# A hybrid attention and SSD kernel: the SSD chunks are turned over, and TensorE's order in the scan is fixed

## The chip, the cores and the metric

The kernel runs on one core of one Trainium2 chip. The metric is the device time of one execution in microseconds. A core has TensorE (PE in the profile, with its weight loads as PEld), VectorE (DVE), ScalarE (ACT), GpSimd (POOL) and SyncE (SP), which issues most of the DMAs. Each engine works through its own queue in order; semaphores make one engine wait for another. TensorE reads its two operands, the stationary and the moving one, from SBUF and writes to PSUM.

## The reference, cut to what matters

Two layers act on 1024 latent tokens and 256 context tokens of width 1024. Layer 0 is windowed attention and is not touched. Layer 1 is a bidirectional Mamba-2 SSD mixer with 8 groups of 4 heads; a head has 64 channels, a state 128 rows. The latent tokens are cut into 8 chunks of 128. In the reference's names, for one direction:

```python
a_cs = jnp.cumsum(da, axis=2)
states = jnp.einsum('bcsgn,bcsgr,bcsgrp->bcgrpn', bm, decay_to_end, xdt)
h = jnp.exp(al)[..., None, None] * h + st                 # scan over the chunks
lmat = jnp.exp(jnp.where(lower, diff, -jnp.inf))
cb = jnp.einsum('bcqgn,bcsgn->bcqsg', cm, bm)
y_diag = jnp.einsum('bcqsg,bcqsgr,bcsgrp->bcqgrp', cb, lmat, xdt)
y_off = jnp.einsum('bcqgn,bcgrpn,bcqgr->bcqgrp', cm, h_prev, jnp.exp(a_cs))
```

and after both directions:

```python
y = y_f + y_b + d_skip * xs
u = rms_normalize((y * silu(z)).reshape(bsz, n, SSD_GROUPS, SSD_WIDTH // SSD_GROUPS))
out = (u.reshape(bsz, n, SSD_WIDTH) * norm_w) @ w_out
```

The gate z, the inputs xs, bm and cm come from one projection of the layer's input; xs, bm and cm go through a convolution over 5 tokens and a SiLU first. The RMS norm of u runs over the 256 channels of a group, token by token.

## The kernel before

All projections are done in split precision: an operand is cut into a high and a low part in fp32r, and three products are summed. The products of the scan are plain fp32; the profile shows each as two passes (two records).

**The stages.** After layer 0 the method `ssd` first runs the front of group 0, then a loop over the groups `g`, in it a loop over the chunks `c`. In the loop over the chunks, `slot` computes chunk `n = 8g + c` of group `g`, and between its parts a call `fill(x)` lets the generator `front(g + 1, ...)` issue projections of the next group. In the last group the generator is `ssd_out`, the output projection. So TensorE always has two kinds of work: the scan of this group, and *fillers* that belong to the next stage. Each filler yields its cost in microseconds (`N512` and `N256`), and `fill` stops at a share of the whole (`FRONT`) given by `SEGS`.

**The front of a group** projects four tiles of 128 channels over all tokens, in the order B, two halves of x, C (L1152 for the latent tokens, L1143 for the context, except C). The result lies in PSUM (`pj2`, two buffers, or `psD`, one buffer) and is convolved by ScalarE (L1034, the middle tap) and VectorE (L1038, the other four), then passed through tanh (L1045) and a product (L1046). B and x are also wanted with the tokens on partitions; for this TensorE transposes the tile into the PSUM space that it came from (L1085), and ScalarE copies it out (L1088). Last comes the gate z (L1177) with the tokens on the output partitions: the stationary operand is the input, the moving one the weight, 256 columns at a time. L1185 and L1188 make the SiLU.

These steps off TensorE are not issued at once. They are put in a `Queue`, `post`, which issues them while fillers run; an entry with a time (`LATE`) is issued that many microseconds of filler later.

**The states.** `states` is a generator for the backward chain: products of B and weighted x (`xw` from GpSimd, L1213) at L1236, a decay of the last state on GpSimd (L1218) and VectorE's sum (L1248), first for the context chunks in both directions, then for the latent chunks from the last to the second. `tick` takes one step of it. The forward state is carried inside `slot` (L1291, L1292).

**A chunk in `slot`** has the queries q on the output partitions. The scores (L1282) are multiplied into the decay matrix M (`fd`, L1286; M comes from `decays`: rows of the cumulated decay loaded from DRAM, one predicated copy L1270 and four exponentials L1272). The two inter-chunk products take C as the stationary operand and the states, 256 columns, as the moving one (L1284, L1285); VectorE scales the result by `eacs`, a factor per token and head (L1295). The diagonal takes M of a head as the stationary operand and 64 channels of x as the moving one (L1311). The skip term, a factor per token and head (`sk`), is multiplied into x on GpSimd (L1306) and added (L1307, L1308). VectorE adds the diagonal (L1320) and multiplies by the gate (L1321); ScalarE sums the squares (L1323), GpSimd takes the power -1/2 (L1324), ScalarE scales (L1329). In the next slot, `tail` transposes the chunk into channel-major form (L1341), ScalarE evicts it with the norm's weight (L1342), and a DMA writes it to `uN_d`.

**What sets the order.** The program is scheduled ahead of time: a timeline model orders the instructions of each engine, so an engine's queue may differ from the program's order. Nothing holds TensorE to the program's order.

**Output projection.** `ssd_out` loads the features from `uN_d` (`oraw`), splits them into high and low (L1529 and the subtraction after it), and multiplies by the weights (L1571). After the scan the rest of it and the final norm run.

## Time and profile before

| | |
|---|---|
| median of 3 runs | 1818.71 us (1813.79 to 1822.03) |
| the profiled execution, its time | 1818.37 us |
| its span, first to last instruction | 1816.6 us |
| mean granted TensorE clock | 0.99 |
| busy share: PE, PEld, DVE, ACT, POOL | 96%, 83%, 64%, 48%, 45% |
| DMA | 227.9 MB, 125 GB/s over the span |
| layer 0 and the joining stage | 0 to about 797 us of the span |
| scan with fronts, groups 0 to 6 | about 857 to 1595 us, 105.5 us per group |
| last group with the output projection | about 1595 to 1700 us |
| rest of the output projection, final norm | about 1700 to 1816 us |

A line of the profile's groups reads: source line, engine, operation, tile written and tiles read, shapes, count, then busy time in us and mean ns of one, then the idle time of the engine before them and what ended it. A matmul's record covers its way through the array, so records overlap; how fast TensorE goes is read from the distance of starts. In the chain of waits a piece has its start, its length and what it was. A line of the busy time by stretches has the stretch, its length, the busy time of PE, PEld, DVE, ACT and POOL with the number of instructions, the granted clock, the DMA engines' share and GB/s.

### The profile page before, as it was taken

To read this page: it belongs to the slowest core of one execution; us is meant where nothing else is said; L and a number is where in the kernel's file an instruction comes from. 1 tells how busy PE (TensorE), PEld (TensorE's weight loads), DVE (VectorE), ACT (ScalarE), POOL (GpSimd) and SP (SyncE) were. 2 spreads that over 40 slices of the span, in tenths; PEclk is the share of its full clock that TensorE was granted. 3 is DMA by queue.
4 is the path that set the end of the run, shared out by engine and by line. 5 is a ranking of instruction groups with operands and counts; after the bars stand their busy time and mean duration, and the time that the engine had idled before them with its cause. 6 is when DMAs were issued, how large, how long until landed. Compare 5 with 4: busy or idle time off the path is not lost.

```text
span 1816.6 us, 29129 instructions
## 1 busy us (share of the span) xinstructions
PE 1749.0 (96%) x10379; PEld 1500.2 (83%) x10379; DVE 1166.0 (64%) x2125; ACT 869.9 (48%) x1895; POOL 811.1 (45%) x1074
## 2 busy tenths in 40 slices
PE   6999998999999899999999999999999999999997
PEld 3797767788889687778898898989889898988886
DVE  3563536786787766675766748567675857766643
ACT  3521235677788766352444434344353434544522
POOL 2441127554456465303454544646454454644311
PEclk9999999999999999999999999999999999999998
DMA  8768865543345445311322323323332322655542
GB/s 296 285 156 255 261 192 138 119 116 99 99 117 132 118 133 195 112 42 52 86 68 79 93 69 88 82 71 79 78 93 78 82 79 74 188 163 179 163 137 70
DMA packets 209393, 227.89 MB, mean 125 GB/s; under 512 B 16096, under 2 KB 149088, under 8 KB 208224
## 3 DMA queue, kind: packets, MB, share of 16 engines
q1 hardware_dynamic: 175184, 207.38, 38.1%
q0 software_dynamic: 34064, 18.65, 5.6%
q8 instruction: 82, 1.34, 0.3%
q14 instruction: 63, 0.52, 0.1%
HBM read 191.14 MB, written 35.13 MB: 125 GB/s over the span
## 4 chain that ended last, share of the span: by engine, by line
PE 83%; DVE 5%; ACT 4%; DMA 4%; issue 3%; POOL 0%; SPq 0%; DVEq 0%; ACTq 0%; POOLq 0%
PE pj L1152 17%; PE pj L1177 10%; PE pj L1571 7%; PE pj L223 6%; PE pj L225 6%; PE pj L224 6%; PE psD L1143 3%; PE pt L694 3%; PE psX L1311 2%; PE pv L701 2%; PE psD L1236 2%; PE pv L700 2%; PE S L669 2%; PE psX L1285 1%; PE S L670 1%
## 5 line engine op out<-in xcount | busy, mean ns | idle before, releaser
L223 PE MATMUL pj<-uH,wh 128*128 128x256 f32 (+1 forms) x652 | 233.5, 358 | 8.1 <-DVE rope_b L532 2.3
L224 PE MATMUL pj<-uL,wh 128*128 128x256 f32 (+1 forms) x652 | 220.1, 338 | 0.0
L225 PE MATMUL pj<-uH,wl 128*128 128x256 f32 (+1 forms) x652 | 220.1, 338 | 0.0
L211 POOL TENSOR_TENSOR wl<-wr,wh 128x512 fp32r<-128x512 f32 x92 | 121.7, 1326 | 97.4 <-ACT wh L209 96.9
L1152 PE MATMUL pj<-uH,wh 128*128 128x512 f32 x480 | 161.4, 410 | 2.0 <-ACT xn L1088 1.2
L1152 PE MATMUL pj<-uH,wl 128*128 128x512 f32 x480 | 158.5, 403 | 0.0
L1152 PE MATMUL pj<-uL,wh 128*128 128x512 f32 x480 | 157.3, 402 | 0.0
L699 DVE TENSOR_TENSOR pl<-pt,ph 128x512 fp32r<-128x512 f32 x168 | 114.2, 687 | 61.3 <-ACT ph L698 60.4
L223 PEld LDWEIGHTS pj<-uH,wh 128*128 128x128 f32 x652 | 124.7, 191 | 34.9 <-issue 8.6
L1177 PE MATMUL pj<-wh,uH 128*128 128x256 f32 x512 | 148.0, 289 | 3.1 <-ACT xn L1088 3.0
L1177 PE MATMUL pj<-wl,uH 128*128 128x256 f32 x512 | 150.7, 294 | 0.0
L1213 POOL TENSOR_TENSOR xw<-xn,dtdec 128x256 f32<-128x256 f32 x144 | 92.9, 649 | 127.1 <-PE psD L1236 108.5
L1177 PE MATMUL pj<-wh,uL 128*128 128x256 f32 x512 | 149.5, 292 | 0.0
L1342 ACT ACTIVATE uT<-psX,nw 128x128 f32<-128x128 f32 x128 | 46.7, 365 | 193.2 <-PE psX L1341 193.1
L225 PEld LDWEIGHTS pj<-uH,wl 128*128 128x128 f32 x652 | 124.4, 191 | 14.8 <-issue 1.7
L673 DVE CUSTOM_DVE_ANT_0 sm<-S,mask,nsink 128x640 f32<-128x640 f32 (+2 forms) x160 | 118.7, 772 | 26.5 <-PE S L670 14.5
L224 PEld LDWEIGHTS pj<-uL,wh 128*128 128x128 f32 x652 | 124.9, 192 | 11.5 <-issue 2.8
L209 ACT CAST wh<-wr 128x512 fp32r<-128x512 f32 (+1 forms) x132 | 84.8, 645 | 102.5 <-PE pj L224 78.7
L698 ACT CAST ph<-pt 128x512 fp32r<-128x512 f32 x168 | 97.5, 585 | 64.5 <-PE pt L694 58.9
L675 ACT ACTIVATE sm<-sm,nm 128x640 f32<-128x640 f32 (+2 forms) x160 | 118.5, 742 | 12.6 <-DVE nm L673 12.3
L1152 PEld LDWEIGHTS pj<-uL,wh 128*128 128x128 f32 x480 | 90.1, 188 | 19.0
L1152 PEld LDWEIGHTS pj<-uH,wh 128*128 128x128 f32 x480 | 89.1, 188 | 19.6 <-ACT bn L1088 2.0
(383 smaller groups left out, 4999.8 us busy)
## 6 DMA issues: line engine op xcount, KB each, us to landing
fd<-acs SPq DMA_DIRECT2D x64, 256.0 KB, 5.0
bd<-acs SPq DMA_DIRECT2D x64, 256.0 KB, 5.2
wr<-w_x SPq DMA_DIRECT2D x31, 512.0 KB, 3.8
wr<-w_sk SPq DMA_DIRECT2D x24, 512.0 KB, 4.0
wr<-wg SPq DMA_DIRECT2D x44, 256.0 KB, 4.6
qs<-q POOLq DMA_DIRECT2D x40, 256.0 KB, 3.9
wr<-wo SPq DMA_DIRECT2D x40, 256.0 KB, 2.7
wada<-w_ad SPq DMA_DIRECT2D x8, 1024.0 KB, 6.4
```

The source lines that it names most:

```text
L211: (eng or nc.vector).tensor_tensor(l, raw, h, op=ALU.subtract)
L223: self.nc.tensor.matmul(ps, lh, rh, start=first and i == 0, stop=False)
L224: self.nc.tensor.matmul(ps, lh, rl, start=False, stop=False)
L225: self.nc.tensor.matmul(ps, ll, rh, start=False, stop=last and i == n - 1)
L673: nc.vector.tensor_tensor_reduce(out=sm[:, :W], in0=Sv, in1=self.mask[:, m0 : m0 + W], scale=-SCALE, scalar=self.nsink[:, 4 * j + r : 4 * ...
L675: nc.scalar.activation(sm[:, :W], sm[:, :W], AF.Exp, bias=nm[:, r : r + 1], scale=-1.0, accum_out=sums[:, r : r + 1])
L698: nc.scalar.copy(ph, ptf)
L699: nc.vector.tensor_sub(pl, ptf, ph)
L1152: nc.tensor.matmul(raw[:, 512 * i : 512 * i + 512], l[:, k, :], r[i][:, k, :], start=k + y == 0, stop=k == KT - 1 and y == 2)
L1177: nc.tensor.matmul(pj[:, c], l, r[:, k, :], start=c % 2 + q + k + y == 0, stop=c % 2 == 1 and q == 1 and k == 3 and y == 2)
L1213: nc.gpsimd.tensor_tensor(xw, X(st, c).rearrange("p (r h) -> p r h", r=R), self.dtdec[:, c, hd(d, g)].unsqueeze(2).broadcast_to([P, R, HP] ...
L1571: nc.tensor.matmul(banks[x], l[:, z, sl], r, start=k == 2 * qs[0] and y == 0, stop=k == 2 * qs[-1] + 1 and y == 2)
```

## The change

- *z turned over* (`front`): the weight tile is stationary, the input moves, 512 columns at a time, so z has channels on partitions. The layout of `w_z` follows. In each tile the latent tokens now come before the context.
- *Chunks turned over* (`scores`, `inter`, `state`, `diagonal` instead of `slot`): y has channels on partitions and queries along the free axis. The inter-chunk products take the states as stationary and C as moving operand, four of 128 columns. The diagonal takes 64 channels of x as the stationary and M as the moving operand; the four heads write to the lower and the upper 64 partitions by turns. The factor per token is no longer per partition, so `exp` of the cumulated decay goes to DRAM (`eacs_d`) and is loaded per chunk, broadcast over 64 partitions (`load_scale`, tile `eb`, two DMAs).
- *Diagonal on VectorE:* the skip term is added into M: four times the identity times `sk`, plus M.
- *Gate on GpSimd:* y times z moves from VectorE to GpSimd. Squares stay on ScalarE; GpSimd adds the two halves and a product with a column of ones gives the sum over channels. The power -1/2 is taken for four chunks at once and written to DRAM (`rn_d`). The chunk is stored before the norm; no transpose is left in the tail.
- *Norm in the output projection:* each feature tile is multiplied on GpSimd by the broadcast row of `rn_d`; the norm's weight is applied in the two splitting steps.
- *TensorE in program order:* `pin` links every TensorE instruction of groups 0 to 6 to the one before it in the program, beginning after the first chunk's scores, state and inter-chunk products.
- *Even fillers, states one by one:* four `fill` calls per chunk with new `SEGS`; the chain of states takes a step whenever `PACE_S` of filler has passed, inside `run`; its rest comes at the end of the last chunk. Transposes of the convolved tiles come `LATE` = 12 (context: `CLATE` = 9.2) us of filler after their tile, and the queue's timed entries are kept sorted.

```diff
-FRONT = 4 * 48 * N512 + 3 * 24 * N256 + 8 * 24 * N256
+FRONT = 4 * 48 * N512 + 3 * 24 * N256 + 4 * 24 * N512
 OUT = 4 * 30 * 3 * N512
 POST = 0.5
 DTLATE = 40.0
-LATE = 3.0
-SEGS = (1.5, 2.0, 2.0, 2.2, 2.2)
+LATE = 12.0
+CLATE = 9.2
+PACE_S = 1.85
+SEGS = (2.6, 2.4, 2.2, 2.25)
...
-            self.late.extend((self.now + f[0], x) for x in f[1])
+            self.late = deque(sorted([*self.late, *((self.now + f[0], x) for x in f[1])], key=lambda v: v[0]))
...
+        for d in range(2):
+            for f in range(2):
+                for r in range(R):
+                    row = 64 * d + 32 * f + r
+                    nc.sync.dma_start(self.eacs_d[r % 2, :, d, r // 2, 512 * f : 512 * f + 512], acs[row : row + 29 : 4, :512])
...
+    def pin(self, first):
+
+        traced = self.nc.cur_bb.bb.instructions
+        start = next(k for k in reversed(range(len(traced))) if traced[k] is first) + 1
+        last = None
+        for i in traced[start:]:
+            if i.engine == mybir.EngineType.PE:
+                if last is not None:
+                    self.tc.add_manual_dep(i, last.name, mybir.DependencyInfo(mybir.DependencyClass.NoSync, mybir.DependencyReason.DATA), reason="pin")
+                last = i
...
-            return [(LATE, steps)]
+            return [(late, steps[::2] + steps[1::2])]
...
+                acc2 = t(pf, [P, CTX], F32, "cctx")
+                post.extend(self.taps(x, raw2, acc2, 0, CTX, CTX) + self.silu(raw2, acc2) + natural(raw2, acc2, [(st[nat[0]][2], 0, 2)], nat[1], 2, CLATE))
+                if kind == 1:
+                    post.append((CLATE, [lambda: st.setdefault("ctx", True)]))
...
-            pj = t(ps, [P, 4, 256], F32, "pj2")
+            pj = t(ps, [P, 2, 512], F32, "pj2")
             for q in range(2):
                 ww = (w0, w)[q]
                 need(ww)
-                for c in range(4):
-                    for k in range(4):
-                        u, v = uH[i][:, 4 * q + k, c * P : (c + 1) * P], uL[i][:, 4 * q + k, c * P : (c + 1) * P]
-                        for y, (l, r) in enumerate(((u, ww["h"]), (u, ww["l"]), (v, ww["h"]))):
-
-                            nc.tensor.matmul(pj[:, c], l, r[:, k, :], start=c % 2 + q + k + y == 0, stop=c % 2 == 1 and q == 1 and k == 3 and y == 2)
-                            yield N256
+                for k in range(KT):
+                    for y, (l, u) in enumerate(((ww["h"], uH), (ww["h"], uL), (ww["l"], uH))):
+                        nc.tensor.matmul(pj[:, q], l[:, k, :], u[i][:, k, :], start=k + y == 0, stop=k == KT - 1 and y == 2)
+                        yield N512
...
+        def load_scale(n):
+            if n < G * NCH:
+                g, c = divmod(n, NCH)
+                x = eb[n] = t(ps2, [P, 2, 2, P], F32, "eb")
+                for f in range(2):
+                    src = self.eacs_d[f : f + 1, g, :, :, c * P : (c + 1) * P].rearrange("o d e q -> o (d e) q")
+                    nc.sync.dma_start(x[64 * f : 64 * f + 64].rearrange("p d e q -> p (d e) q"), src.broadcast_to([64, R, P]))
...
+        def scores(n, st, cur):
             g, c = divmod(n, NCH)
             cs = slice(c * P, (c + 1) * P)
             pcb = t(ps, [P, 512], F32, "psX")[:, :P]
             nc.tensor.matmul(pcb, st["bT"][:, cs], st["cT"][:, cs], start=True, stop=True)
+            M = cur["M"]
+            y2 = cur["y2"] = t(ps2, [P, 2, 2, P], F32, "y2")
+            sk = t(ps2, [P, R + 1], F32, "sk")
+            dg, sk = sk[:, R:], sk[:, :R]
+            nc.vector.tensor_tensor_reduce(out=y2[:, 0, 0], in0=pcb, in1=self.ident, scale=1.0, scalar=0.0, op0=ALU.mult, op1=ALU.add, accum_out=dg)
+            nc.vector.scalar_tensor_tensor(sk, in0=self.dtb[:, c, 4 * g : 4 * g + 4], scalar=dg, in1=self.dsk[:, 4 * g : 4 * g + 4], op0=ALU.mult, op1=ALU.add)
             nc.vector.tensor_tensor(M, M, pcb.unsqueeze(1).broadcast_to([P, R, P]), op=ALU.mult)
+            for r in range(R):
+                nc.vector.scalar_tensor_tensor(M[:, r], in0=self.ident, scalar=sk[:, r : r + 1], in1=M[:, r], op0=ALU.mult, op1=ALU.add)
+
+        def inter(n, st, cur):
+            g, c = divmod(n, NCH)
+            cs = slice(c * P, (c + 1) * P)
+            po = t(ps, [P, 2, 2, P], F32, "psX")
+            for d, h in enumerate((cur["hf"], st["hb"][c])):
+                for e in range(2):
+                    nc.tensor.matmul(po[:, d, e], flat(h)[:, e * P : (e + 1) * P], st["cT"][:, cs], start=True, stop=True)
+            y2 = cur["y2"]
+            nc.vector.tensor_tensor(y2, po, eb.pop(n), op=ALU.mult)
+            y = cur["y"] = t(ps2, [P, 2, P], F32, "yt")
+            cur["yadd"] = nc.gpsimd.tensor_tensor(y, y2[:, 0], y2[:, 1], op=ALU.add).ins
+
+        def state(n, st, cur):
+            g, c = divmod(n, NCH)
+            cur["hf"] = st["hf"]
             if c < NCH - 1:
+                xw = xweight(st, g, c, 0)
                 S = t(ps, [P, 512], F32, "psX")
                 hn = t(ps2, [P, R, HP], F32, "hf")
                 decay(hn, st["hf"], g, c, 0)
+                yield
+                nc.tensor.matmul(S[:, :256], B(st, c), flat(xw), start=True, stop=True)
                 nc.vector.tensor_add(hn, hn, S[:, :256].rearrange("p (r h) -> p r h", r=R))
                 st["hf"] = hn
+            yield
+
+        def diagonal(n, st, cur):
+            g, c = divmod(n, NCH)
+            cs = slice(c * P, (c + 1) * P)
+            M, y, y2 = cur["M"], cur["y"], cur["y2"]
             yd = t(ps, [P, 512], F32, "psX")
             for r in range(R):
+                e, f = divmod(r, 2)
+                nc.tensor.matmul(yd[64 * f : 64 * f + 64, e * P : (e + 1) * P], X(st, c)[:, r * HP : (r + 1) * HP], M[:, r], start=True, stop=True)
+            yadd = nc.vector.tensor_add(y, y, yd[:, :256].rearrange("p (e q) -> p e q", e=2))
+            nc.gpsimd.tensor_tensor(y, y, st["sz"][c], op=ALU.mult)
+            nc.sync.dma_start(self.uN_d[g][:, :, cs].rearrange("e p n -> p e n"), y)
+            nc.scalar.activation(y2[:, 0], y, AF.Square, scale=1.0 / 16.0)
+            sq = t(ps2, [P, P], F32, "sq")
+            nc.gpsimd.tensor_tensor(sq, y2[:, 0, 0], y2[:, 0, 1], op=ALU.add)
+
+            def tail():
+                pt = t(ps, [P, 512], F32, "psX")
+                nc.tensor.matmul(pt[:, :1], sq, self.ones[:, :1], start=True, stop=True)
+                if c % 4 == 0:
+                    self.ss = t(ps2, [P, 4], F32, "ss", 2)
+                ss = self.ss
+                nc.scalar.activation(ss[:, c % 4 : c % 4 + 1], pt[:, :1], AF.Identity, bias=self.eps4)
+                if c % 4 == 3:
+                    nc.gpsimd.tensor_tensor(ss, ss, self.mhalf, op=ALU.pow)
+                    nc.sync.dma_start(self.rn_d[g][c // 4].rearrange("o (c p) -> p (o c)", c=4), ss)
+
+            return tail, yadd.ins
 
...
-        st["xw"] = xweight(st, 0, 0, 0)
-        self.tail = None
+        cur = {"M": decays(0)}
+        scores(0, st, cur)
+        for _ in state(0, st, cur):
+            pass
+        inter(0, st, cur)
+        tail = None
+        traced = nc.cur_bb.bb.instructions
+        first = traced[-1]
...
+                    self.pin(first)
...
+                        if g < G - 1 and "ctx" in nst:
+                            chain = chain or states(g + 1, nst)
+                            if spent - mark > PACE_S and (steps < 4 or 1 in nst):
+                                next(chain, None)
+                                steps += 1
+                                mark = spent
...
+                    if n + 1 < G * NCH:
+                        load_scale(n + 2)
+                    if n + 1 < G * NCH:
+                        with self.tc.issue_after(cur["yadd"]):
+                            offset(n + 1)
+                    ntail, ydone = diagonal(n, st, cur)
+                    if tail:
+                        tail()
+                    tail = ntail
+                    load_rows(n + 2, 0)
+                    if n + 1 < G * NCH:
+                        with self.tc.issue_after(ydone):
+                            cur = {"M": decays(n + 1)}
+                    fill(0)
+                    if n + 1 == G * NCH:
+                        run(total * (c + 1) / NCH)
+                        break
+                    if c == NCH - 1:
+                        while not all(x in nst for x in ("bT", "cT", 1)) or not nst["sz"]:
+                            post.pop()
+                        st = nst
+                    scores(n + 1, st, cur)
+                    fill(1)
+                    fs = state(n + 1, st, cur)
+                    next(fs)
+                    if c < NCH - 1:
+                        inter(n + 1, st, cur)
+                        fill(2)
+                        for _ in fs:
+                            pass
+                    else:
+                        fill(2)
+                        for _ in chain:
+                            pass
+                        next(fs)
+                        inter(n + 1, st, cur)
+                    fill(3)
...
+                if k % 2 == 0:
+                    nc.sync.dma_start(scales[k // 2 % 2][:, k // 4 % 2 * 512 :][:, :512], self.rn_d[k // 2][i].broadcast_to([P, 512]))
...
+                def scale():
+                    nc.gpsimd.tensor_tensor(feats[n], feats[n], scales[k // 2 % 2][:, k // 4 % 2 * 512 :][:, :512], op=ALU.mult)
+
+                def high():
+                    nc.scalar.activation(hi, feats[n], AF.Copy, scale=self.nw[:, k : k + 1])
 
                 def low():
-                    nc.vector.tensor_sub(lo, feats[n], hi)
+                    nc.vector.scalar_tensor_tensor(lo, in0=feats[n], scalar=self.nw[:, k : k + 1], in1=hi, op0=ALU.mult, op1=ALU.subtract)
                     ready.add(order[n])
 
-                post.extend([lambda: nc.scalar.copy(hi, feats[n]), low])
+                post.extend([scale, high, low])
```

130 lines of the change are left out of this document (30 added, 100 removed).

## The prediction

> **What bounds the kernel now.** I read the page's head first, then busy time by stretches of one group of the scan stage, then the chain of waits.
>
> ```profile
> span 1816.6 us, 29129 instructions
> PE 1749.0 (96%) x10379; PEld 1500.2 (83%) x10379; DVE 1166.0 (64%) x2125; ACT 869.9 (48%) x1895; POOL 811.1 (45%) x1074
> ```
>
> ```profile
> 1067.07:1172.61 105.54, 104.80 (x652) 93.79 (x651) 71.96 (x123) 45.34 (x106) 53.67 (x75) 1.00 0.29 78
> ```
>
> The columns after the length are PE, PEld, DVE, ACT and POOL busy, then clock and DMA. TensorE is busy 104.8 of 105.5 us at full clock, so a group idles only 0.74 us. A busy PE may still be a slow one, so I look at the cadence.
>
> ```profile
> 1156.49 2.63 PE pj L1177 x22
> 1159.12 0.22 PE psX L1282 x2
> 1159.34 0.43 PE psD L1236 x2
> 1159.77 0.43 PE psX L1284 x2
> ```
>
> ```profile
> 1126.93 0.40 PE L1152 MATMUL pj<-uL,wh 128*128 128x512 f32 x1
> 1127.16 1.00 PE L1311 MATMUL psX<-xn,fd 128*128 128x64 f32 x8
> 1127.97 0.48 PE L1152 MATMUL pj<-uL,wh 128*128 128x512 f32 x1
> 1128.29 0.39 PE L1152 MATMUL pj<-uH,wl 128*128 128x512 f32 x1
> 1128.52 0.27 PE L1341 MATMUL psX<-ident,y 128*128 128x128 f32 x1
> 1128.55 0.47 PE L1152 MATMUL pj<-uH,wl 128*128 128x512 f32 x1
> 1128.86 0.63 PE L1152 MATMUL pj<-uH,wh 128*128 128x512 f32 x2
> ```
>
> The first fence is the chain of waits (start, length, what). It is nothing but TensorE, one piece starting where the last ended: 22 products of 256 columns take 2.63 us, 0.1195 each. The second is TensorE's timeline, with starts in the first column. A 512-column product takes 0.23 (1128.29 to 1128.52). From 1126.93 to 1128.29 there are two such products and the eight passes of the diagonal, so these cost 1.36 - 0.46 = 0.90 us. A transpose costs 1128.86 - 1128.29 - 0.46 = 0.11. Work put between the projections costs its own passes and no more, so in this stage a pass saved is time saved, and a wait of TensorE is time lost. There are almost no waits to remove.
>
> **The change part by part: TensorE's work.** The gate z is turned over: per group 192 products of 256 columns become 96 of 512.
>
> ```profile
> 1717.40 11.04 PE pj L1571 x48
> ```
>
> This piece of the chain (output projection, a new stationary tile each time) gives 0.230 per 512 columns. So 192 x 0.1195 = 22.9 becomes 96 x 0.230 = 22.1 us: 0.8 to 0.9 less per group, and over eight groups -7.0 us. It can hardly be worth less than 4.
>
> The diagonal: four products of 64 columns, bound by loading M, become four of 128 columns with X stationary, 64 columns wide, two on the lower and two on the upper half of the output partitions. A fp32 pass over 128 columns is 0.11 (L1282, two in 0.22). If the halves run side by side, 8 passes take 4 x 0.11 = 0.44; one after the other 0.88. The trace has one form that lies side by side, the adaLN strips at L187 (32 columns, four strips), and one that is 64 wide but alone, L942:
>
> ```profile
> 158.95 0.39 PE L225 MATMUL pj<-uH,wl 128*128 128x512 f32 x1
> 159.27 1.06 PE L187 MATMUL aps<-wl,cs 128*32 128x512 f32 x8
> 160.26 0.39 PE L223 MATMUL pj<-uH,wh 128*128 128x256 f32 x1
> 160.49 0.28 PE L224 MATMUL pj<-uL,wh 128*128 128x256 f32 x1
> ```
>
> ```profile
> 710.14 0.39 PE L225 MATMUL pj<-uH,sm 128*128 128x512 f32 x1
> 710.37 0.28 PE L942 MATMUL pt<-uH,wdth 128*64 128x256 f32 x1
> 710.49 0.28 PE L942 MATMUL pt<-uL,wdth 128*64 128x256 f32 x1
> 710.60 0.39 PE L225 MATMUL S<-uH,sm 128*128 128x512 f32 x1
> ```
>
> L187's eight passes of 512 columns would be 8 x 0.43 = 3.4 us in a row (a pass over 256 columns is 0.215 by L1284). They take 160.49 - 158.95 - 0.23 - 0.12 = 1.19, two passes' time (0.86) and 0.33 besides: four strips do run at once, and going in and out of that form costs 0.33 per visit. L942 shows no such toll (0.23, 0.12, 0.11 between starts). So the diagonal is worth 0.44 (no toll), 0.77 (L187's) or 0.88 + 0.33 = 1.21 (toll, and one after the other). I take 0.77, since only L187 puts its strips beside each other. Against 0.90 that is -0.13 x 64 chunks = -8.3 us, with ends of -29 and +20.
>
> The Trainium skill, "TensorEngine Tiling (Array Packing)", Tiling Modes, says that changing the tiling mode drains the engine; L187's 0.33 us agrees and L942's starts do not. The same page's Performance Considerations recommend this very swap for a moving side of 64 columns or fewer, at up to twice the speed; by that sentence alone the diagonal would be 0.45 and the sum 20 us lower.
>
> Inter-chunk products: four of 128 columns (8 x 0.11 = 0.88) for two of 256 (0.43 + 0.43): +0.02 x 64 = +1.3 us. The tail: two transposes (0.22) go, one product of a single column comes; its two passes still load 128 columns, as L1311's passes do at 0.90 / 8 = 0.11: 0.22, so nothing. Scores, states and the other projections keep their shapes. TensorE's sum: -7.0 - 8.3 + 1.3 = -14.0 us.
>
> **What is moved to other engines.** Per chunk VectorE loses the gate product (L1321) and gets four adds of the scaled identity into M, each 128 columns.
>
> ```profile
> L1038 DVE SCALAR_TENSOR_TENSOR cctx<-psD,cw,cctx 128x254 f32<-128x254 f32 (+1 forms) x12 | 5.7, 471 | 0.0
> ...
> L1321 DVE TENSOR_TENSOR y<-y,sz 128x256 f32<-128x256 f32 x8 | 4.3, 540 | 0.2
> L1248 DVE TENSOR_TENSOR hb<-hb,psD 128x256 f32<-128x256 f32 x8 | 3.4, 419 | 14.1 <-PE psD L1236 13.6 <-POOL hb L1218 0.5
> ...
> L1302 DVE SCALAR_TENSOR_TENSOR sk<-dtb,dg,dsk 128x4 f32<-128x4 f32 x8 | 1.7, 215 | 0.0
> ```
>
> The same operation is 215 ns on 4 columns and 471 on 254, so about 340 on 128: four are 1.4 us, less 0.54, at most +0.8 per chunk and +6.6 on 72 us per group. That hides under TensorE's 104 as long as no deadline is missed (a rival below). GpSimd and ScalarE get lighter:
>
> ```profile
> L1308 POOL TENSOR_TENSOR y<-y,xs 128x256 f32<-128x256 f32 x8 | 5.9, 735 | 0.4
> L1306 POOL TENSOR_TENSOR xs<-xn,sk 128x256 f32<-128x256 f32 x8 | 5.8, 726 | 9.2 <-DVE sk L1302 9.2
> L1218 POOL TENSOR_TENSOR hb<-hb,eal 128x256 f32<-128x256 f32 x8 | 5.1, 643 | 0.2 <-DVE hb L1248 0.2
> ```
>
> ```profile
> fd<-acs SPq DMA_DIRECT2D x64, 256.0 KB, 5.0
> ```
>
> L1308, L1306 and three of four powers go, one gate product and a 128-column add come. ScalarE loses two evictions and a scaling. The new scale rows (256 KB per chunk on SP, as much as `fd`) are asked for two chunks ahead, with the DMA engines 0.29 busy. All that is hidden; without cover the rows would cost what `fd` takes to land, 5.0 us a chunk, but a chunk (13 us) lies between request and use.
>
> **The pinned order.** In groups 0 to 6 each TensorE instruction waits for the one before it in the program; what is late next holds all fillers behind it. I price four places.
> - *Group's end:* the chain's last product stands about 1 us of filler behind the one before, and the new chunk's products need its result. It waits for GpSimd's decay (L1218, 0.64) and VectorE's add (L1248, 0.42). Between 0 and 2.3 us (a tap of 1.27 us ahead in the queue); I take 0.7: 7 x 0.7 = +5.
> - *Entry:* chunk 0's diagonal is now the first pinned instruction and needs M, some 2.5 us of VectorE work after its scores, less 1.3 us of products between: +1.5 (0 to 4).
> - *Output projection:* each feature gets a scale row and a GpSimd product ahead of the split:
>
> ```profile
> L1471 POOL TENSOR_TENSOR xn<-xn,bn 128x512 f32<-128x512 f32 x7 | 11.1, 1589 | 9.4 <-ACT bn L1470 8.9
> ```
>
> at 1.6 us x 32 = 51 us on GpSimd in a stage of 155 us; only the first feature is exposed: +1.5 (0 to 4).
> - *Transposes of the conv'd tiles:* now 12 us of filler after the tile's last product, about 16.7 us of time (104 us per group for 74.6 of filler by the code's own count).
>
> ```profile
> 1085.15 1.20 ACT L1034 ACTIVATE bT<-pj,cb,cw 128x1024 f32<-128x1024 f32 x1
> ```
>
> ```profile
> 1086.57 1.27 DVE L1038 SCALAR_TENSOR_TENSOR bT<-pj,cw,bT 128x1022 f32<-128x1022 f32 x1
> ...
> 1095.22 1.23 DVE L1046 SCALAR_TENSOR_TENSOR bT<-pj,bT 128x1024 f32<-128x1024 f32 x1 [0.43 <-ACT pj L1045]
> ```
>
> ScalarE starts the tile at 1085.2 and VectorE ends it at 1096.5: 11.3 us, plus the handover to ScalarE. That leaves 4 to 5 us: +0 beyond today's 0.74 idle.
>
> Sum: -14.0 + 5 + 1.5 + 1.5 = -6 us. The profiled run is 1818.4 us (span 1816.6 and 1.8 around it), within 0.4 of the median of 1818.7, so **1812 us**.
>
> **The rivals.**
> 1. *No toll.* The two halves run side by side without the 0.33, as L942 suggests: 64 x 0.33 = 21 less, 1791. Against it: L942 lies on one half alone. Chance 0.24.
> 2. *VectorE comes late (the other side).* In the half of a group with the three conv'd tiles VectorE has little room:
>
> ```profile
> 1118.00:1148.00 30.00, 29.39 (x182) 25.97 (x181) 25.71 (x43) 17.09 (x39) 14.37 (x20) 1.00 0.37 100
> 1188.00:1208.00 20.00, 20.00 (x117) 17.52 (x116) 17.57 (x27) 11.20 (x27) 7.83 (x11) 1.00 0.26 79
> ```
>
>    43.3 of 50 us here, 0.87, and 0.06 more with the adds (0.8 of 13 us): 0.93. If each of three tiles comes one 1.27 us tap late at its pinned transpose, 3 x 1.27 x 7 = 27 us: 1839. It decides once the 11.3 us from tile to transpose exceed 16.7. Against it: that margin. Chance 0.17.
> 3. *The halves don't overlap,* and pay the toll: 1.21 instead of 0.77, +28: 1840. Against it L187's four strips at once. Chance 0.09.
>
> **How the numbers follow.** The forecast has 0.50, with its own range of 1803 to 1823 (group ends free, or at 2.3 us). About 0.5%, some 9 us, is what a measurement of this kernel tells from no change: faster is below 1809.6, slower above 1827.8. Of the forecast's 0.50 I put 0.21 below that bound and 0.29 within. Faster: 0.21 + 0.24 = 0.45; same 0.29; slower 0.17 + 0.09 = 0.26. The range reaches to all three rivals: 1789 to 1841.
>
> **What would show it.** z at 0.23 per product and 96 per group; the diagonal's passes in pairs, and from the filler before to the second filler after 0.77 beyond them (0.44: rival 1; 1.21: rival 3); idle time of TensorE at the group's ends from `hb`, one to two us; idle time ahead of the transposes or the diagonal, released by VectorE, for rival 2. A group of 103 to 104 us fits the forecast. Wrong would be a TensorE that waits more than 3 us a group, or a visit to the halves that costs what no row here shows.

## The result and the profile after

The changed kernel takes 1877.6 us (median of 4, 1871.9 to 1880.4); the kernel before takes 1818.9 beside it. The ratio is 1.032 (95% interval 1.029 to 1.036): slower by 59 us, where 1812 was predicted. The profiled execution took 1878.8 us, its span is 1877.0, and the mean granted TensorE clock 0.974 in place of 0.990.

Where the time went is read from the start of a chunk's diagonal on TensorE, which both kernels have. The stretches below are cut there; all are in us.

| stretch | before | after | difference |
|---|---|---|---|
| start to the first diagonal (chunk 0) | 862.9 | 873.9 | +11.0 |
| chunk 0 to chunk 48 (groups 0 to 5) | 635.6 | 631.1 | -4.5 |
| chunk 48 to 56 (group 6) | 104.6 | 124.8 | +20.2 |
| chunk 56 to 63 (group 7) | 86.0 | 97.4 | +11.4 |
| chunk 63 to the end | 127.5 | 149.8 | +22.3 |

Busy time after the change, for one period of the pinned groups (105 us, cut at a transpose) and for the last three of those stretches, which are group 6, group 7 and the rest. Columns as in the prediction: PE, PEld, DVE, ACT, POOL, then clock, DMA share, GB/s.

```profile
1010.29:1115.22 104.93, 104.20 (x586) 85.87 (x587) 77.87 (x149) 38.48 (x81) 51.62 (x68) 1.00 0.44 102
1505.02:1629.80 124.78, 112.62 (x587) 91.06 (x586) 89.44 (x153) 43.83 (x89) 63.79 (x75) 0.93 0.56 152
1629.80:1727.20 97.40, 89.24 (x436) 69.69 (x435) 58.27 (x110) 33.28 (x67) 49.78 (x52) 0.96 0.62 158
1727.20:1877.00 149.80, 125.45 (x713) 109.53 (x712) 71.22 (x86) 44.66 (x70) 50.28 (x39) 0.91 0.36 121
```

The same three last stretches before the change:

```profile
1498.50:1603.10 104.60, 103.67 (x643) 92.19 (x642) 81.31 (x137) 53.88 (x120) 55.75 (x74) 1.00 0.52 146
1603.10:1689.10 86.00, 86.00 (x422) 72.08 (x422) 53.66 (x93) 37.57 (x86) 39.53 (x50) 1.00 0.55 168
1689.10:1816.60 127.50, 112.16 (x674) 99.67 (x672) 57.82 (x76) 40.32 (x67) 27.70 (x25) 0.94 0.36 114
```

In groups 1 to 5 TensorE idles as little as before (0.73 us a group). In group 6 it idles 12.2 us: this is the sign of being wrong that the prediction named, a TensorE that waits more than 3 us a group. From group 6 on it idles 44.7 us in place of 16.3 (lengths less busy), and its busy time grows by 25 us although the work is much the same: the clock falls. What holds TensorE in group 6 stands in GpSimd's timeline (start, length, what, and in brackets the idle time before and its end):

```profile
1592.70 2.50 POOL L1589 TENSOR_TENSOR oraw<-oraw,bT 128x512 f32<-128x512 f32 x2 [3.64 <-DMA bT<-rn]
1595.16 0.62 POOL L1236 TENSOR_TENSOR hb<-hb,eal 128x256 f32<-128x256 f32 x1
...
1597.99 3.41 POOL L1589 TENSOR_TENSOR oraw<-oraw,cT 128x512 f32<-128x512 f32 x2
1601.37 0.61 POOL L1236 TENSOR_TENSOR hb<-hb,eal 128x256 f32<-128x256 f32 x1
...
1609.51 1.26 POOL L1589 TENSOR_TENSOR oraw<-oraw,bT 128x512 f32<-128x512 f32 x1 [5.37 <-issue]
1610.73 0.62 POOL L1236 TENSOR_TENSOR hb<-hb,eal 128x256 f32<-128x256 f32 x1
```

L1589 is the norm's product for a feature of the output projection, L1236 a decay of group 7's chain of states. The products wait for loads, the decays stand behind them, and TensorE, in program order, stands behind the chain:

```profile
1596.29 0.70 PE L1254 MATMUL psD<-xw,bn 128*128 128x256 f32 x2 [2.45 <-DVE hb L1266]
...
1597.16 0.63 PE L1194 MATMUL pj<-uL,wh 128*128 128x512 f32 x1
1597.59 0.63 PE L1194 MATMUL pj<-uH,wl 128*128 128x512 f32 x1
1598.01 0.63 PE L1194 MATMUL pj<-uH,wh 128*128 128x512 f32 x1
...
1604.03 1.19 PE L1254 MATMUL psD<-xw,bn 128*128 128x256 f32 x2 [2.43 <-DVE hb L1266]
...
1607.40 0.40 PE L1194 MATMUL pj<-uH,wh 128*128 128x512 f32 x1
1607.64 0.39 PE L1194 MATMUL pj<-uL,wh 128*128 128x512 f32 x1
1607.87 0.40 PE L1194 MATMUL pj<-uH,wl 128*128 128x512 f32 x1
...
1611.85 1.22 PE L1254 MATMUL psD<-xw,bn 128*128 128x256 f32 x2 [3.59 <-DVE hb L1266]
```

A wait can cost twice: after 2.45 us of idling the next 512-column products start 0.43 us apart (1597.16, 1597.59, 1598.01), and only 3.4 us after the second wait do they start 0.23 to 0.24 apart again (1607.40, 1607.64, 1607.87). The Trainium skill, "TensorE: Matmul & The Clock Gate", Part 1, says that the clock falls to half once TensorE has been idle for a window of about 3.4 us; the half rate agrees (0.43 against 0.23), but here gaps of 2.4 us suffice. The length of a gap alone doesn't decide it: ahead of the same product of layer 0, 1.37 us of idling were followed by 3 us at half rate in e3 (618.1 us), and 1.42 and 1.69 us by none in e2 (617.7) and the kernel before (622.8). Over the span the clock's missing share is 1877 x 0.026 = 49 us against 18 before (1817 x 0.010): up to 31 of the 60 us.

The second place is SP's queue, late in the output projection:

```profile
1749.04 0.37 SPq L1369 DMA_DIRECT2D rn<-ss  x1
1757.20 0.32 SPq L1577 DMA_DIRECT2D cT<-rn  x1
1757.62 9.65 SPq L1558 DMA_DIRECT2D wr<-w_sk  x3
```

The factors are stored (L1369), and SP waits to load them back (L1577). The store takes 8 us; the weights behind it are issued at 1757.6, ScalarE splits them at 1764.6, and TensorE starts again at 1765.7 after 7.09 us:

```profile
1764.61 1.04 ACT L1563 CAST wh<-wr 128x1024 fp32r<-128x1024 f32 x1 [9.26 <-DMA wr<-w_sk]
...
1765.71 0.80 PE L1640 MATMUL pj<-uH,wh 128*128 128x512 f32 x1 [7.09 <-ACT wh L1563]
```

### The profile page after: what moved, and what is told of

It reads as the page before. It is cut to its first block, busy times and chain, and to the rows that moved or that the text cites. A ratio compares the mean times of both kernels' runs of the same rounds, so it can differ in the third digit from the quotient of the medians.

```text
span 1877.0 us, 28458 instructions
## 1 busy us (share of the span) xinstructions
PE 1771.5 (94%) x9863; PEld 1452.7 (77%) x9863; DVE 1228.8 (65%) x2315; ACT 816.0 (43%) x1699; POOL 839.0 (45%) x1058
## 5 line engine op out<-in xcount | busy, mean ns | idle before, releaser
L1231 POOL TENSOR_TENSOR xw<-xn,dtdec 128x256 f32<-128x256 f32 x144 | 101.5, 711 | 143.5 <-PE psD L1254 53.9
L1161 PE MATMUL pj<-uH,wh 128*128 128x512 f32 x480 | 162.0, 409 | 0.0
L1161 PE MATMUL pj<-uH,wl 128*128 128x512 f32 x480 | 160.4, 403 | 0.0
L1161 PE MATMUL pj<-uL,wh 128*128 128x512 f32 x480 | 159.9, 405 | 0.0
L225 PEld LDWEIGHTS pj<-uH,wh 128*128 128x128 f32 x652 | 124.6, 191 | 35.0 <-issue 7.8
L675 DVE CUSTOM_DVE_ANT_0 sm<-S,mask,nsink 128x640 f32<-128x640 f32 (+2 forms) x160 | 118.8, 772 | 25.9 <-PE S L672 13.8
L211 ACT CAST wh<-wr 128x512 fp32r<-128x512 f32 (+1 forms) x132 | 84.8, 645 | 103.0 <-PE pj L226 77.7
L700 ACT CAST ph<-pt 128x512 fp32r<-128x512 f32 x168 | 97.4, 585 | 64.3 <-PE pt L696 58.8
L1194 PE MATMUL pj<-uH,wh 128*128 128x512 f32 x256 | 118.3, 462 | 1.8 <-ACT xn L1105 1.8
L1329 POOL TENSOR_TENSOR yt<-y 128x256 f32<-128x256 f32 x64 | 48.7, 761 | 153.4 <-DVE y L1327 153.3
L1194 PE MATMUL pj<-uH,wl 128*128 128x512 f32 x256 | 105.7, 413 | 0.0
L1366 ACT ACTIVATE ss<-psX,eps 128x1 f32<-128x1 f32 x64 | 16.5, 259 | 202.5 <-PE psX L1362 202.5
L1194 PE MATMUL pj<-uL,wh 128*128 128x512 f32 x256 | 104.4, 408 | 0.0
```

The costliest lines, as they stand in the source:

```text
L211: nc.scalar.copy(h, raw)
L225: self.nc.tensor.matmul(ps, lh, rh, start=first and i == 0, stop=False)
L675: nc.vector.tensor_tensor_reduce(out=sm[:, :W], in0=Sv, in1=self.mask[:, m0 : m0 + W], scale=-SCALE, scalar=self.nsink[:, 4 * j + r : 4 * ...
L700: nc.scalar.copy(ph, ptf)
L1161: nc.tensor.matmul(raw[:, 512 * i : 512 * i + 512], l[:, k, :], r[i][:, k, :], start=k + y == 0, stop=k == KT - 1 and y == 2)
L1194: nc.tensor.matmul(pj[:, q], l[:, k, :], u[i][:, k, :], start=k + y == 0, stop=k == KT - 1 and y == 2)
```

## The experiments

"The changed kernel" is 1.0321 times the kernel before; each ratio below is against runs of the kernel before on the same chip, with its 95% interval. The runs are spread over four chips, so where two experiments ran on different ones, a difference of a few us is better read from the ratios. The profiled executions differ too: the stretch ahead of the first product of group 0, the same work in all of them, takes 749.6 to 756.9 us in the runs where it was measured.

**Is it the pinned order, or the norm's step?** e1 and e2 drop the pin wholly or for group 6; e3 and e4 take the norm's step apart.

```diff
-                    self.pin(first)                       # e1
+                if g == G - 2: self.pin(first)            # e2, at the loop's head
-                post.extend([scale, high, low])           # e3, and no load of rn
+                post.extend([high, low])
+                for x in scales: nc.vector.memset(x, 1.0) # e4, and no load of rn
```

> The changed kernel without the pinned order: TensorE's order in groups 0 to 6 is the planner's again, all else as changed. Theory A (the loss comes from the norm's step in the output projection: its GpSimd products wait for DMAs at the head of GpSimd's queue, and the decays of the chain of states stand behind them): the late decays stay, TensorE can only partly work around them; the 11 us at the entry into the scan go; 1855 to 1872 us. Theory B (the pinned order turns a small lateness into TensorE idling; unpinned it would be filled): 1820 to 1835 us.

> The changed kernel with the order pinned in groups 0 to 5 only; group 6, where the first features of the output projection are fetched, is left to the planner. Theory A: the products of the norm still stand ahead of the decays; of the 20 us lost in group 6 at most half comes back: 1862 to 1875 us. Theory B: group 6's 20 us come back, and the 11 us after it in group 7 with them, and part of the clock: 1830 to 1845 us. The entry (11 us) stays as it is by both.

> The changed kernel without the norm's factor in the output projection: no rows of rn are loaded and no product is made on GpSimd; the features go into the split unnormalized, so the norm over a group's 256 channels is left out of the result (its sums, powers and stores remain). Theory A: the loss after group 5 goes nearly whole (49 of the 60 us; the entry's 11 stay): 1820 to 1833 us, and the first diagonal of group 7 within 8 us of where it was before the change (1603). Theory B: the pinned order has its price wherever something is late; 1850 us or more.

> As the changed kernel, but the norm's product on GpSimd takes a constant tile of ones in place of the rows of rn, which are not loaded (so the norm is left out of the result; the sums, powers and stores of rn remain). It tells the two halves of theory A apart. If the way of the factor through DRAM is what is late (SP waits for the store of rn, and weights and features stand behind it): as without the norm's step, 1820 to 1833 us. If the place of the products in GpSimd's queue, where each waits for its feature's load, is enough: 1850 to 1872 us.

Measured: e1 1906.8 us (1.0501, 1.0479 to 1.0523), e2 1887.4 (1.0390, 1.0373 to 1.0407), e3 1852.3 (1.0197, 1.0176 to 1.0219), e4 1868.5 (1.0286, 1.0268 to 1.0305). As an account of the loss theory B falls: without the pin the kernel is 29 us slower still, a group taking 111 us (999.3 to 1554.3 for five) in place of 104.93. In groups 1 to 5 the pin was not the loss; it saved 6 us a group of the new program, and its first diagonal comes at 873.9 us, e1's at 889.8. At the end it does cost: in e1 group 6 takes 118.0 us in place of 124.8, and from group 7's first diagonal to the end it takes 238.6 in place of 247.2. e3 gives back 25 us: the norm's step is a cause, but not of all 49. Only e4 lies where theory A put it: e1 and e2 are slower than both theories had it, and e3's time lies in the range of B. e4 against e3 puts 16 us on the products on GpSimd, against the changed kernel 9 on loading the factors back from DRAM (their store is still made in e4).

**What is left in e3.** The store of `rn` still runs in e3. DMA traffic of e3 from 1618 to 1638 us, in 40 slices of 0.5 us (busy tenths, then GB/s), and ScalarE:

```profile
DMA  4587942426495599999999100702100135400000
GB/s 81 157 227 205 271 105 85 57 35 59 92 134 102 197 305 336 370 337 234 135 12 14 8 0 0 24 5 57 39 28 9 45 123 169 138 0 0 0 0 0
```

```profile
1633.06 1.33 ACT L1586 ACTIVATE uH<-oraw,nw 128x512 fp32r<-128x512 f32 x2 [9.13 <-DMA oraw<-uN]
```

The store is issued at 1621.9, two loads of features at 1622.8. From 1628 to 1633 almost nothing moves, and then the features are there. The store writes a column of factors as 512 pieces of 4 bytes. So e5 takes the store out of e3, and e6 keeps the whole computation and writes rows:

```diff
-                    nc.sync.dma_start(self.rn_d[g][c // 4].rearrange("o (c p) -> p (o c)", c=4), ss)
+                        nc.tensor.transpose(pr[:4, :P], ss, self.ident)      # one chunk later
+                        nc.scalar.copy(rr, pr[:4, :P])
+                        nc.sync.dma_start(self.rn_d[g][c // 4].rearrange("o (c p) -> (o c) p", c=4), rr)
```

> As e3_no_norm_step (no factor in the output projection, so the norm over a group's channels is left out of the result), and the store of rn is gone too: 512 pieces of 4 bytes for every four chunks. In e3's trace the store is issued at 1621.9 us, two loads of features behind it at 1622.8 land only at 1633, while the DMA engines move almost nothing from 1628 to 1633, and ScalarE waits 9.1 us for them with the weights' split behind it. Theory C: this store stalls the DMA queue by 5 us or more each time, and in group 6 and after somebody waits for the loads behind it: 1825 to 1840 us, the stretch from group 7's first diagonal to the end 215 to 225 us (236 in e3, 213.5 before the change). Theory D: the loads are late for their own size or their place in the queue, the store has nothing to do with it: 1846 to 1856 us.

> The whole changed kernel with one thing else: the factors of four chunks are transposed by TensorE (128x4 to 4x128), copied by ScalarE and stored as four rows of 512 bytes in place of 512 pieces of 4 bytes, one chunk later in the program. (Tile yt has two buffers in place of three, to make room.) Theory C: the stalls of the DMA queue go, 10 to 20 us come back against 5 us of more work on TensorE and ScalarE: 1858 to 1870 us. Theory D: 1876 to 1884 us.

e5: 1841.9 (1.0137, 1.0112 to 1.0162), 10 us under e3, short of what theory C expected. e6: 1854.7 (1.0194, 1.0170 to 1.0217): 23 us back with the 2 KB stored as rows, more than expected; no run separates the shape of the store from its place one chunk later. In the profiles 17.3 of the 22 us lie behind group 7's first diagonal (229.9 us in place of 247.2), and 4.3 lie ahead of the first diagonal, where the edit changes nothing. Theory D falls. SP's waits for this store (us in total, times, longest), in the changed kernel from 1590 to 1780 us and in e6 from 1590 to 1760:

```profile
SPq L1577 <- DMA rn<-ss: 14.7, 2, 7.7
```

```profile
SPq L1589 <- DMA rn<-rr: 3.8, 2, 2.9
```

The Trainium skill, "DMA: Bandwidth & Descriptors", Specifications, says that transfers under 512 bytes are read, modified and written back, and its section "Queues, rings and completion order" that a DMA's signal lands only after every earlier write of its engine. Loads behind the store that land 10 us after their issue agree with the second; whether the 4-byte pieces are read first no run here shows.

**The entry.** e7 undoes the later transposes in group 0 (and lets group 0's chain of states start only when the context is there), e8 combines it with e6 and VectorE in GpSimd's place.

```diff
+        late, clate = (LATE, CLATE) if g else (3.0, 3.0)                    # e7, e8
-                    nc.gpsimd.tensor_tensor(feats[n], feats[n], scales...
+                    nc.vector.tensor_tensor(feats[n], feats[n], scales...   # e8, with e6
```

> The whole changed kernel, but in the front of group 0 the transposes of the convolved tiles come 3 us of filler after their tile, as before the change, in place of 12 and 9.2; from group 1 on all is as changed. Theory E: the 11 us at the entry are the chain of states of group 0, which starts 12 us of filler late and runs out serially with TensorE waiting for every step; the first diagonal then comes at 863 to 866 us (873.9 in the changed kernel, 862.9 before) and the time is 1866 to 1871 us. Rival: the entry is bound by the new order of context and latent tokens or by the chunk's own start: first diagonal at 871 or later, 1875 us or more.

> The whole changed kernel with three edits: entry as in e7, row store as in e6, and the norm's product of each feature on VectorE in place of GpSimd. If the three costs are separate (10 us at the entry, 10 to 20 for the store, up to 16 for the products on GpSimd by e3 against e4): 1832 to 1850 us. If the products on VectorE only move the waiting for a load from the head of GpSimd's queue to the head of VectorE's, where the chain of states needs its sums: 1850 to 1865 us.

e7: 1878.3 (1.0330, 1.0305 to 1.0356), nothing. Theory E falls: from the first product of group 0 to the first diagonal it takes 119.3 us, as in the changed kernel (118.8; before 106.9). e8: 1858.7 (1.0216, 1.0199 to 1.0233), no better than e6: on VectorE the products wait ahead of the chain's sums instead (one waits 3.27 us for its load until 1608.3, and a sum stands behind it).

**The chain's place in the queues, and the order at the entry.** e9 puts the features' products behind the chain, e10 projects the context first in group 0, e11 does both; all on top of e6.

```diff
+                    with self.tc.issue_after(self.cdec):     # the chain's last decay
                         nc.gpsimd.tensor_tensor(feats[n], feats[n], scales...
+                    with self.tc.issue_after(self.cadd):     # its last sum
                         nc.vector.scalar_tensor_tensor(lo, in0=feats[n], ...
+            if nat and g == 0:                               # e10: context ahead of latent tokens
+                raw2 = t(ps, [P, 512], F32, "psD")[:, :CTX]
```

> As e6_row_store (1854.7 us), and the norm's product and the low part of each feature are queued on GpSimd and VectorE behind the last decay and the last sum of the chain of states of group 7. Theory F (twelve products of features stand between the seven last decays in GpSimd's queue, so every step of the chain comes late and the pinned TensorE with it): group 6 (from its first diagonal to group 7's) goes from 124.3 us to 105 to 111, the first features then come some 2 to 5 us late for the output projection, and with the clock 1836 to 1846 us. Rival G (the chain is late for something else, as in e5_no_norm_no_store where no product is made and group 6 still takes 109.5, or the late features cost as much as is won): 1850 us or more.

> As e6_row_store, but in the front of group 0 the context of the second x tile is projected before its latent tokens, as before the change, with the transposes 3 us after their tile. e7 showed that the 3 us alone do nothing: the chain of states started at 835 us in both, 12 us later than before the change, behind the context's transposes at 826 to 829, and ran its last seven steps with TensorE waiting. If the order of context and latent tokens is the cause, the chain starts near 823 us again, the first diagonal comes at 858 to 864 us (869.6 in e6) and the time is 1843 to 1850 us. If not: 868 us or more and 1852 us or more.

> The edits of e9 and e10 together. If they are separate costs, both gains add: 1826 to 1838 us. If the end of the kernel (from group 7's first diagonal on: 229.9 us in e6, 213.5 before the change) is what remains, this stays 6 us or more above the kernel before the change, for its groups 1 to 5 save about 3 us.

e9: 1850.1 (1.0189, 1.0168 to 1.0210). Its group 6, group 7 and rest:

```profile
1502.80:1605.60 102.80, 101.71 (x576) 83.91 (x575) 77.10 (x146) 38.67 (x83) 49.73 (x65) 1.00 0.55 154
1605.60:1724.60 119.00, 109.95 (x525) 87.09 (x524) 89.80 (x126) 45.35 (x84) 78.87 (x69) 0.94 0.65 189
1724.60:1848.30 123.70, 106.40 (x638) 93.57 (x638) 59.57 (x77) 38.47 (x63) 36.82 (x33) 0.93 0.36 114
```

Theory F is right about the place: group 6 falls from 124.3 to 102.8 us, at full clock. But GpSimd is now busy 78.9 of 119 us in group 7 (49.3 of 89.2 in e6), and from chunk 56 to the end it takes 242.7 us in place of 229.9: more than half is given back, and the time lies in rival G's range. Not all of group 6's 21.5 us belong to the products: e5, which makes none, still takes 109.5 there, and e15 (below), which makes none either and has the low parts behind the chain, takes 103.0. So some 6.5 us are the place of the low parts on VectorE. e10: 1853.2 (1.0202, 1.0171 to 1.0233), not to be told from e6. e11: 1845.7 (1.0165, 1.0145 to 1.0185), 4.4 us under e9, and not the 1826 to 1838 of two gains that add. From the first product of group 0 to the first diagonal e10 takes 115.5 and e11 112.1 us, with the same code there (120.0 in e6): the order is 4 to 7 of the 12 us at the entry, though the time shows it in one of two pairs only.

**What the last groups still lose.** All on top of e11: no skip term (e12), an earlier boundary for the features (e13), six pinned groups (e14), no norm in the output projection (e15).

```diff
-                nc.vector.scalar_tensor_tensor(M[:, r], in0=self.ident, scalar=sk[:, r : r + 1], ...)  # e12
+                    if n < len(jobs) - 3: self.cdec, self.cadd = dec, add                              # e13
```

> As e11_row_chain_context (1845.7 us), but VectorE's four adds of the scaled identity into M are left out, so the skip term is left out of the result. The prediction counted these adds as hidden. If they are hidden in groups 1 to 5, those stay at 104.9 us each (within 0.2). In group 7 e11's TensorE waited for them and for what stands behind them on VectorE (the diagonal: 2.05, 0.54, 0.59, 0.84, 0.84 us). Theory H (VectorE is late in the last group, where features and weights are split beside the scan): from group 7's first diagonal to the end 232 to 238 us (244.3 in e11) and 1834 to 1841 us. Rival I (the last group waits for weights and features, the adds only show it): 1843 us or more.

> As e11, but the features' products and low parts may stand behind the fourth last step of the chain of states in place of the last. Rival I (what group 6 won is given back because the features come late): group 6 102.8 to 108 us, and from group 7's first diagonal to the end 228 to 238 us in place of 244.3; 1834 to 1842 us. Theory H: no gain, 1844 to 1852 us.

> As e11, with TensorE's order pinned in groups 0 to 5 only. In the changed kernel this cost 10 us (e2). If that was the planner counting on features that came late, and they still come behind the chain, TensorE may now fill group 6 with products of the output projection as before the change: 1830 to 1842 us. If the planner's order of the last groups is bad by itself: 1848 to 1862 us.

> The context of group 0 first as in e11, the low parts of the features behind the chain as in e9, and no norm at all in the output projection (no store of rn, no rows, no product, so the result isn't normalized over a group's channels). It is the changed kernel with every cost named so far taken out. If nothing else is lost: 1812 to 1822 us (the kernel before less 3 to 5 us of groups 1 to 5, plus what the clock lost). If the last group has a cost of its own (VectorE and the order of the chunk turned over): 1826 to 1838 us.

e12: 1829.3 (1.0073, 1.0048 to 1.0097), 16 us under e11. But of it only 2.4 us lie after chunk 56, where theory H had put them; 10 lie in groups 0 to 5, which were to stay at 104.9. Its groups take 103.4:

```profile
1069.20:1172.60 103.40, 103.35 (x591) 86.10 (x590) 68.45 (x115) 38.36 (x84) 51.57 (x69) 1.00 0.39 102
```

The transposes of the convolved tiles show how, in TensorE's groups of the six pinned groups, first the changed kernel (idle before them 3.1 and 1.2 us), then e12 (none):

```profile
L1102 PE MATMUL pj<-ident,cacc 128*128 128x128 f32 x96 | 13.1, 280 | 3.1 <-DVE cacc L1052 2.4
L1102 PE MATMUL pj<-ident,bT 128*128 128x128 f32 x49 | 6.9, 281 | 1.2 <-DVE bT L1052 1.2
```

```profile
L1103 PE MATMUL pj<-ident,cacc 128*128 128x128 f32 x104 | 13.5, 273 | 0.0
L1103 PE MATMUL pj<-ident,bT 128*128 128x128 f32 x48 | 6.2, 272 | 0.0
```

Part of the lateness is no idle time in the records: the step from the filler before to the first transpose shrinks, on average, from 0.63 to 0.23 us at three places a group, which makes 1.2 of the 1.5 us. e13: 1847.9 (1.0167; what the end wins, 236.8 us in place of 244.3, group 6 loses, 111.7 in place of 102.8) and e14: 1856.1 (1.0215, 1.0178 to 1.0251): neither the boundary nor the pin of group 6 is what is left. e15: 1832.0 (1.0080, 1.0060 to 1.0100): the norm still costs 14 us when its store and its place are mended.

**Closing the account.** e16 leaves out both the norm and the four adds; e17 computes everything and moves other work, the low part of the weights, from VectorE to GpSimd.

```diff
-                nc.vector.tensor_sub(w["l"], raw, w["h"])
+                (nc.gpsimd if g else nc.vector).tensor_tensor(w["l"], raw, w["h"], op=ALU.subtract)  # e17
```

> As e15_no_norm_chain_context (1832.0 us; no norm over a group's channels in the result), and VectorE's four adds of the scaled identity into M are left out too (no skip term in the result). It closes the account: e15 against e11 gave 13.7 us, e12 against e11 16.3. If the two costs are separate: 1814 to 1819 us, as fast as the kernel before with groups 1 to 5 at 103.4 us. If both took the same lateness away: 1824 to 1831 us.

> As e11_row_chain_context (1845.7 us), whole, but the low parts of the front's weights from group 1 on are made by GpSimd in place of VectorE (six of 1.5 us a group on VectorE). If VectorE's lateness at the pinned transposes is the 1.5 us a group that e12 showed: groups 1 to 5 at 103.4 to 104.2 us and 1835 to 1842 us. If GpSimd, with up to 3 us for each behind a wait for the weights, holds up its decays instead: 104.9 us or more a group and 1846 us or more.

e16: 1817.3 (0.9995, 0.9980 to 1.0010), the time of the kernel before: the two costs add. e17: 1858.6 (1.0225, 1.0199 to 1.0252), 106.8 us a group. One such part takes 2.45 us on GpSimd, and TensorE now waits for `xw`, which stands behind it (twice a group, 1.8 us together):

```profile
L1083 POOL TENSOR_TENSOR wl<-wr,wh 128x1024 fp32r<-128x1024 f32 x6 | 14.7, 2452 | 7.8 <-ACT wh L1079 7.8
```

No version that computes everything beats the kernel before; the best is e11, 1845.7 us.

## Why the prediction was wrong

The account of the 59 us, by runs: 23 for the store in small pieces (e6), 9 for the chain's place and the entry's order (e11 against e6), 16 for VectorE's adds (e12), 14 for the rest of the norm's way (e15); they add to 62, and e16, with all of them taken out, is 60 us faster than the changed kernel. By the ratios, which allow for the chip, they are 23, 5, 17 and 15.

- **The step that failed most is the output projection:** "only the first feature is exposed: +1.5 (0 to 4)". It compared sums, 51 us of GpSimd in 155, and not places in a queue. The products wait for loads and stand ahead of the chain's decays. And the store of `rn`, named among the changes, was given no price at all: the prediction weighed the 256 KB of scale rows of a chunk, and not these 2 KB. Together 37 us and more, by e6 and e15, in place of 1.5.
- **Hidden VectorE work:** four adds were put at 1.4 us a chunk and measured 10.2 / 8 = 1.3, so the duration was right:

```profile
L1317 DVE SCALAR_TENSOR_TENSOR fd<-ident,sk,fd 128x128 f32<-128x128 f32 x32 | 10.2, 380 | 0.1
```

  "That hides under TensorE's 104" was wrong by 1.5 us a group. This is rival 2, whose condition came true in a smaller size: three tiles late by some 0.4 us each, not 1.27. The margin of 4 to 5 us between tile and transpose was taken from the kernel before, where VectorE did not have the adds. In the changed kernel a tile takes 14.5 to 15.3 us from ScalarE's start to VectorE's end (995.78 to 1010.24, 1014.15 to 1029.47, 1034.60 to 1049.12) and not 11.3, and the transposes come 15.4 to 15.7 us after its last product and not 16.7, so nothing of the margin is left.
- **TensorE's sum was right.** e12's group has 103.35 us of TensorE in place of 104.80: -1.45, against -14.0 / 8 = -1.75 (e12 also makes the two small transposes of the row store). The toll of the column form is there, as L187 suggested:

```profile
1017.25 0.39 PE L1161 MATMUL pj<-uH,wh 128*128 128x512 f32 x1
1017.57 0.66 PE L1352 MATMUL psX<-fd,xn 128*64 128x128 f32 x8
1018.16 0.38 PE L1362 MATMUL psX<-ones,sq 128*128 128x1 f32 x2
1018.40 0.48 PE L1161 MATMUL pj<-uH,wh 128*128 128x512 f32 x1
1018.72 0.62 PE L1161 MATMUL pj<-uL,wh 128*128 128x512 f32 x2
```

  From 1017.25 to 1018.72 are two fillers (0.46), the tail's two passes (0.22) and the diagonal: 0.79 where 0.77 was taken. Rivals 1 (0.44) and 3 (1.21) fall. The halves do run side by side: the eight records, 0.27 long each, fit into 0.66, so the last starts 0.39 after the first, where eight passes one after the other would need 7 x 0.11 = 0.77. z takes 0.23 to 0.24 per product (1607.40, 1607.64, 1607.87), as predicted.
- **Group's end:** 0.7 us were set for it. From the starts in groups 0 to 5 the three steps at a group's end (the chain's last product, the new chunk's state product and its inter-chunk products) take 2.07 us beyond the fillers; elsewhere they take 0.44 + 0.44 + 0.90, so the wait is 0.3. Mis-sized, in the good direction.
- **Entry:** +1.5 (0 to 4) was the price of the first diagonal's wait for M. Measured are 12 us, and for something else: in the changed kernel TensorE idles 4.39 us before the context's transposes, and the last seven steps of group 0's chain run with nothing between, from 857.8 to the first diagonal at 873.9:

```profile
829.09 0.69 PE L1102 MATMUL psD<-ident,cctx 128*128 128x128 f32 x2 [4.39 <-DVE cctx L1052]
```

  The order of context and latent tokens, which the prediction had passed over, is 4 to 7 of it. The adds are 2.3 in one pair (109.8 us in e12, 112.1 in e11) and 0.3 in the other (112.2 in e16, 112.5 in e15). The rest is open.
- **The pinned order** was priced as a cost alone. e1 shows that the new program needs it in groups 1 to 5, and that it costs some 15 us from group 6 on.
- **The clock** has no term in the sum. Up to 31 of the 60 us are idle time charged a second time; the account by runs above has them inside its terms.

What stays open: e16 takes 227.6 us from chunk 56 to the end, the kernel before 213.5, and wins it back in groups 0 to 6. No run takes that apart.

## What to carry to other kernels

Price a moved step by what it waits for and by what stands behind it in each queue, the SP queue and the smallest store among them; a sum of busy time over a stage shows none of this. Work is hidden only if the deadlines that it shifts have room in the new program: where TensorE's order is fixed, 0.4 us of lateness at three places a group was most of 1.5 us. Store a per-token column as rows.

## What the hardware showed unexpectedly

- A store of 2 KB in 512 pieces of 4 bytes held SP's next dependent load for up to 7.7 us, and the same bytes in four rows for at most 2.9. In e3 two loads queued 0.9 us behind such a store landed 10 us after their issue.
- An idle gap of 2.4 us can be enough to halve TensorE's rate for about 3 us; even 1.37 us was in e3, and 1.42 us at the same place in e2 was not.
- Two 64-column halves do run side by side in fp32, but entering and leaving that form costs some 0.35 us (0.79 less four passes of 0.11), as it does with four strips of 32.
- GpSimd's product of y and the gate took 1.05 us in the mean of a pinned group (0.73 to 2.29 over the run), where the sum in L1308 of the kernel before took 0.74 (median) on the same shape. What the difference comes from no run here shows.
